# Recurrent mixer: row halves in turns into two banks, triangle inversions on GpSimd, and the convolution norm over four token tiles

## The chip, the cores and the metric

One core of a Trainium2 chip runs the whole kernel. The metric is the device time of one execution in microseconds: the median of three runs before was 3958.29 us (3955.69 to 3967.6). The engines are TensorE (PE in the profile; PEld are its weight loads), VectorE (DVE), ScalarE (ACT), GpSimd (POOL) and SyncE (SP), which issues most DMAs. PSUM has eight banks into which TensorE writes; the kernel names them by use.

## The reference, cut to what matters

Three blocks follow one another on a sequence of 1024 tokens of width 1024: four mixers, then a recurrent mixer (RWKV-7) beside a convolution group and a feed-forward layer, then a gated block with dilated attention. The change lies in the second block, between its input projection and its output projection.

```python
def rwkv7_recurrence(r, decay, k, v, a_vec, b_vec):
    ...
    def step(S, inp):
        r_t, w_t, k_t, v_t, a_t, b_t = inp
        sa = jnp.einsum('bhvk,bhk->bhv', S, a_t)
        S = S * w_t[:, :, None, :] + sa[..., :, None] * b_t[:, :, None, :] + v_t[..., :, None] * k_t[:, :, None, :]
        y = jnp.einsum('bhvk,bhk->bhv', S, r_t)
        return S, y
    ...

def conformer_conv_group(u, conv_w, conv_b, conv_ln_g, conv_ln_b):
    h = u[..., :D_CONV] * jax.nn.sigmoid(u[..., D_CONV:])
    h = lax.conv_general_dilated(...) + conv_b
    mu = jnp.mean(hf, axis=-1, keepdims=True)
    var = jnp.mean(jnp.square(hf - mu), axis=-1, keepdims=True)
    hn = (hf - mu) * lax.rsqrt(var + LN_EPS) * conv_ln_g + conv_ln_b
    return jax.nn.silu(hn).astype(u.dtype)
```

The recurrence has 8 heads of 64 channels and one state of 64x64 for each head. The kernel doesn't step through the 1024 tokens: it works in chunks of 64, for which the updates inside a chunk become a unit lower triangular system.

## The kernel before, in words

The large projections (helper line L251) are float32 products made of three calls on split operands. The recurrent stage uses plain float32 calls of `nc.tensor.matmul`; the trace shows each as two matmul instructions, called two passes here.

The stage takes eight token blocks j of 128 tokens, two chunks of 64 each. 512 channels stand as 4 pairs of 128 partitions; a head has 64 of them, so two heads share a pair, one on partitions 0 to 63 and one on 64 to 127 (the row halves). Five generators make the work of a block:

- `rwkv_prep(j)` loads r, k and v, makes the decay and the gate (L1336: products with `wup` on either row half into bank s; GpSimd L1340 to L1385), scales the operands, and forms the masked products of both chunks, `gs` (L1403 on TensorE, L1405 on VectorE), four groups of four calls, a group for each chunk and row half. Its ten work tiles `wk` are there once, so one block's preparation follows the other's.
- `rwkv_solve(j)` inverts the 16x16 triangles on the diagonal. DMAs bring them from `gs` through DRAM into a tile of 64 lanes by 256; GpSimd copies it (L1423) and sets the diagonal (L1424); then 14 steps, each a product (L1428) and a sum (L1430) of 14 to 56 elements a lane, each waiting for the one before; a transposing copy (L1433); and DMAs bring the result back as T16 and P16.
- `rwkv_pre(j)` transposes (L1457), forms ET from `gs` and T16 (L1465), takes three steps of a series with P16 (L1473) between which x1 is made (L1480), and ends with VU (L1488) and X (L1493). Each product is eight calls of 64 columns for each of the two chunks, each chunk on its own row half.
- `rwkv_chain(j)` carries the state through both chunks (L1516 to L1541), with Sc on GpSimd (L1518), and `rwkv_out(j)` normalises the output O (scaled on GpSimd in L1564) and gates it.

`rwkv` weaves chain(i), out(i-1), pre(i+1), solve(i+2) and prep(i+3) for i from -3 to 8, by the counts in `RW`; at i = -3 the generator `conv_ln` is woven in, which normalises the convolution output in eight tiles of 128 tokens (L1212 to L1234): transposes into a bank t, statistics on VectorE, a chain of small VectorE operations for the inverse root (L159 to L168), the normalisation out of the bank (L1221), transposes back, ScalarE, and two GpSimd operations. Weaving sets the order in which instructions are written; the framework's scheduler then reorders them by its own estimate of times. 88 filler products (L172) keep their places in the program order.

Banks: mm and o have one each, f (fillers) one, s two, t three. Products of `rwkv_prep` go to s, those of `rwkv_pre` and the norm's transposes to t.

## Time and profile before

| | |
|---|---|
| median of three runs | 3958.29 us |
| the profiled execution, its own time | 3958.3 us |
| its span | 3956.6 us |
| PE busy in the span | 3795.8 us (96%) |
| DVE, ACT, POOL busy | 2112.9 (53%), 1231.0 (31%), 540.1 us (14%) |
| the stage of the change in the span | 1116 to 1491 us |

A row of the chain gives shares of the span along the chain of work that ended last. A row of the stretches gives busy times and instruction counts in a window, and the granted clock of TensorE as a share of full speed (1.00 is 2.4 GHz). A row of waits names the waiting engine and line, and what released it. A timeline row gives start, duration, engine, line, operation, output and inputs, and in brackets idle time before it. Busy times of TensorE in a group of lines count each instruction from start to end, though instructions overlap. In the stage, inversion steps and work tiles share names, since their memory is cut out of weight tiles: "ws" and "kb" are such cuts.

### The profile page before, as it was taken

How to read it: one execution, taken by the hardware profiler on the slowest of the kernel's cores; microseconds unless marked ns; L12 is line 12 of the kernel's file. 1: busy time of each engine (PE TensorE's matmuls, PEld its weight loads, DVE VectorE, ACT ScalarE, POOL GpSimd, SP SyncE). 2: the span in 40 equal slices, each digit the busy share in tenths (PEclk: the TensorE clock that was granted, in tenths of full speed). 3: DMA queues.
4: the chain of work that ended last, by engine and by line, in shares of the span. 5: the costliest groups of instructions: out<-in, count | busy, mean ns of one | idle time of the engine just before them, and what ended most of it. 6: DMA issues, size and time to landing. Idle time of an engine off the chain costs nothing.

```text
span 3956.6 us, 52689 instructions
## 1 busy us (share of the span) xinstructions
PE 3795.8 (96%) x20288; PEld 3149.7 (80%) x20288; DVE 2112.9 (53%) x4845; ACT 1231.0 (31%) x2521; POOL 540.1 (14%) x825
## 2 busy tenths in 40 slices
PE   7999999799988989999999999999999999999998
PEld 6788888687867777888888888878788888888887
DVE  5356568678977865544444554444433443433155
ACT  4444435542233334222212242333322111121232
POOL 1011124300033411000000011111101211210000
PEclk9999998899978999999999999999999999999999
DMA  5321342431211133111111132111133222211143
GB/s 148 122 65 51 82 138 65 150 114 57 91 55 38 40 104 120 48 54 43 54 43 54 54 121 60 41 58 54 54 107 96 62 64 58 78 49 43 59 150 127
DMA packets 318636, 303.75 MB, mean 77 GB/s; under 512 B 50670, under 2 KB 260402, under 8 KB 318386
## 3 DMA queue, kind: packets, MB, share of 16 engines
q1 hardware_dynamic: 318386, 300.39, 24.5%
q8 instruction: 160, 2.62, 0.3%
q14 instruction: 90, 0.74, 0.1%
HBM read 234.27 MB, written 61.34 MB: 75 GB/s over the span
## 4 chain that ended last, share of the span: by engine, by line
PE 87%; DVE 6%; DMA 3%; ACT 1%; issue 1%; SPq 1%; POOL 1%; DVEq 0%; ACTq 0%; POOLq 0%
PE mm L251 71%; PE s L1809 2%; DMA wraw<-in_w_in_dram 1%; PE s L532 1%; PE t L568 1%; PE o L1831 1%; PE s L1990 1%; PE o L1883 1%; DVE ws L738 1%; PE t L213 1%; PE o L578 1%; PE o L579 1%; SPq L1439 1%; PE s L1403 0%; PE s L531 0%
## 5 line engine op out<-in xcount | busy, mean ns | idle before, releaser
L251 PE MATMUL mm<-ahi,whi 128*128 128x512 f32 x2464 | 967.2, 394 | 0.0
L251 PE MATMUL mm<-alo,whi 128*128 128x512 f32 x2464 | 965.5, 392 | 1.3 <-DVE alo L218 1.3
L251 PE MATMUL mm<-ahi,wlo 128*128 128x512 f32 x2464 | 964.3, 392 | 1.9 <-DVE wlo L184 1.9
L184 DVE TENSOR_TENSOR wlo<-wraw,whi 128x1024 fp32r<-128x1024 f32 (+2 forms) x300 | 358.2, 1231 | 361.1 <-PE mm L251 337.6
L251 PEld LDWEIGHTS mm<-ahi,wlo 128*128 128x128 f32 x2464 | 464.7, 189 | 98.4 <-DVE wlo L184 2.6
L251 PEld LDWEIGHTS mm<-ahi,whi 128*128 128x128 f32 x2464 | 465.8, 189 | 96.3 <-issue 0.4
L251 PEld LDWEIGHTS mm<-alo,whi 128*128 128x128 f32 x2464 | 465.1, 189 | 96.7 <-DVE alo L218 2.2
L183 ACT ACTIVATE whi<-wraw 128x1024 fp32r<-128x1024 f32 (+2 forms) x300 | 302.9, 1055 | 760.2 <-DMA wraw<-in_w_ff_dram 315.1
L251 PE MATMUL mm<-whi,ahi 128*128 128x512 f32 (+2 forms) x1088 | 400.2, 371 | 21.1 <-ACT whi L183 8.2
L251 PE MATMUL mm<-whi,alo 128*128 128x512 f32 (+2 forms) x1088 | 399.0, 368 | 1.6 <-DVE alo L218 1.6
L251 PE MATMUL mm<-wlo,ahi 128*128 128x512 f32 (+2 forms) x1088 | 400.4, 368 | 0.1
L251 PEld LDWEIGHTS mm<-whi,ahi 128*128 128x128 f32 x1088 | 206.6, 190 | 57.1 <-ACT whi L183 8.7
L1683 DVE TENSOR_TENSOR xm<-xm,mm 128x512 f32<-128x512 f32 x256 | 173.6, 684 | 119.8 <-PE mm L251 119.5
L251 PEld LDWEIGHTS mm<-wlo,ahi 128*128 128x128 f32 x1088 | 206.5, 190 | 35.2 <-issue 3.8
L251 PEld LDWEIGHTS mm<-whi,alo 128*128 128x128 f32 x1088 | 206.0, 189 | 35.2 <-issue 2.5
L251 PE MATMUL mm<-whi,ah 128*128 128x512 f32 x512 | 202.3, 395 | 0.0
L251 PE MATMUL mm<-wlo,ah 128*128 128x512 f32 x512 | 202.1, 395 | 0.0
L251 PE MATMUL mm<-whi,al 128*128 128x512 f32 x512 | 202.1, 395 | 0.0
L1170 DVE SCALAR_TENSOR_TENSOR cva<-cvh,vecs,cva 128x1022 f32<-128x1022 f32 (+29 forms) x120 | 145.4, 1262 | 0.2
L1665 DVE TENSOR_TENSOR fr<-fr 128x512 f32<-128x512 f32 x64 | 44.4, 694 | 154.0 <-ACT fr L1664 154.0
L207 POOL TENSOR_SCALAR x<-x,rT 128x1024 f32<-128x1024 f32 x16 | 20.9, 1307 | 752.3 <-PE mm L251 676.8
L1815 POOL TENSOR_SCALAR mS<-mS,s 128x256 f32<-128x256 f32 x128 | 60.8, 478 | 405.2 <-DVE s L1814 337.8
(576 smaller groups left out, 5761.2 us busy)
## 6 DMA issues: line engine op xcount, KB each, us to landing
wraw<-in_w_in_dram SPq DMA_DIRECT2D x41, 1024.0 KB
wraw<-in_w_ff_dram SPq DMA_DIRECT2D x32, 1024.0 KB
wraw<-in_w_in_dram SPq DMA_DIRECT2D x59, 512.0 KB
wraw<-in_w_out_dram SPq DMA_DIRECT2D x24, 1024.0 KB
gv<-go SPq DMA_DIRECT2D x32, 256.0 KB
vl<-gv SPq DMA_DIRECT2D x16, 512.0 KB
wraw<-in_w_proj_a_dram SPq DMA_DIRECT2D x8, 1024.0 KB
wraw<-in_w_proj_b_dram SPq DMA_DIRECT2D x8, 1024.0 KB
```

The source lines that it names most:

```text
L183: nc.scalar.activation(hi, src, AF.Copy)
L184: nc.vector.tensor_tensor(lo, src, hi.bitcast(F32), op=OP.subtract)
L213: nc.tensor.transpose(q[:, 128 * j:128 * j + 128], xn[:, (k + j) * 128:(k + j + 1) * 128], self.ident)
L251: nc.tensor.matmul(out, lhs[a][:, kl, ls], rhs[b][:, kr, rs], start=first and n == 0, stop=last and n == tot - 1)
L532: nc.tensor.matmul(q[:, :b - a], self.Q[0:64, h, qs], kl, start=False, stop=True)
L568: nc.tensor.transpose(t[:w, (2 * j + s) * 128:(2 * j + s + 1) * 128], Ps[s][:, k:k + w], c.ident)
L578: nc.tensor.matmul(o[:, :256], v[:w, 0:128], ph[:w, sl], start=first, stop=last, skip_group_check=True)
L1170: nc.vector.scalar_tensor_tensor(a[:, 30 - j:], h[:, 0:994 + j], wj, a[:, 30 - j:], op0=OP.mult, op1=OP.add)
L1665: nc.vector.tensor_tensor(r, r, r, op=OP.mult)
L1683: nc.vector.tensor_tensor(xm[t][:, ns], xm[t][:, ns], q, op=OP.add)
L1809: nc.tensor.matmul(q[:, :256], qk[:, a, qcol], qk[:, b, kcol], start=n == 0, stop=n == 2)
L1815: nc.gpsimd.tensor_scalar(S_, S_, r, 1.0, op0=OP.mult, op1=OP.mult)
```

## The change

Three edits, all in the second block. First, six kinds of products of `rwkv_prep` and `rwkv_pre` (wup, gs, ET, x1, VU with X) take two banks at once and are written so that calls on rows 0 to 63 and on rows 64 to 127 follow in turns, each half into its own bank. x1 of both chunks is made after the first step of the series, where chunk 1's stood after the second. Second, the 28 inversion steps of a block and the copy behind them are issued on GpSimd instead of VectorE. Third, `conv_ln` takes four token tiles at a time: their transposed values are copied to SBUF by ScalarE, their variances collected in one tile, one inverse root is taken for four, and the normalisation runs in place in SBUF. The weave count of the norm rises from 16 to 24.

```diff
@@ -1128,7 +1128,7 @@
 
 
 FN = 384
-RW = dict(chain=(9, "010000"), out=(4, "0000"), pre=(15, "100111011010001"), solve=(10, ""), prep=(7, "00010000001"), ln=16, weave=1)
+RW = dict(chain=(9, "010000"), out=(4, "0000"), pre=(15, "100111011010001"), solve=(10, ""), prep=(7, "00010000001"), ln=24, weave=1)
 
 
 class Block2:
@@ -1203,37 +1203,46 @@
                 yield
 
     def conv_ln(self, tmp):
+
         c, nc = self.c, self.c.nc
         g, b = c.vecs["conv_ln_g"], c.vecs["conv_ln_b"]
-        for t in range(8):
-            ts = slice(t * 128, t * 128 + 128)
-            q = c.psum("t")
-            for i in range(4):
-                nc.tensor.transpose(q[:, 128 * i:128 * i + 128], self.cv[:, i, ts], c.ident)
-            yield
-            st = c.sm([128, 6], pool=tmp)
-            nc.vector.bn_stats(st, q)
-            mv = c.sm([128, 2], pool=tmp)
-            nc.vector.bn_aggr(mv, st)
-            rs = c.sm([128, 1], tag="cl", pool=tmp)
-            c.rsqrt(rs, mv[:, 1:2], 1.0, 1e-5, "cl", tmp)
-            x = tmp.tile([128, 512], F32, tag="O", name=c.nm("lnx"), bufs=2)
-            nc.vector.tensor_scalar(x, q, mv[:, 0:1], rs, op0=OP.subtract, op1=OP.mult)
-            yield
-            q = c.psum("t")
-            yf = tmp.tile([128, 512], F32, tag="Pc", name=c.nm("lny"), bufs=3)
-            y = yf.rearrange("p (i t) -> p i t", i=4)
-            for i in range(4):
-                nc.tensor.transpose(q[:, 128 * i:128 * i + 128], x[:, 128 * i:128 * i + 128], c.ident)
-            for i in range(4):
-                nc.scalar.activation(y[:, i], q[:, 128 * i:128 * i + 128], AF.Identity, bias=b[:, i:i + 1], scale=g[:, i:i + 1])
-            yield
-
-            nc.scalar.activation(x, yf, AF.Tanh, scale=0.5)
-            nc.gpsimd.tensor_scalar(x, x, 0.5, 0.5, op0=OP.mult, op1=OP.add)
-            nc.gpsimd.tensor_tensor(yf, yf, x, op=OP.mult)
-            nc.sync.dma_start(self.catT[512:1024, ts].rearrange("(i p) t -> p i t", p=128), y)
-            yield
+        for t0 in (0, 4):
+            xs = []
+            mv = c.sm([128, 4, 2], tag="cmv", bufs=2, pool=tmp)
+            for k in range(4):
+                ts = slice((t0 + k) * 128, (t0 + k) * 128 + 128)
+                q = c.psum("t")
+                for i in range(4):
+                    nc.tensor.transpose(q[:, 128 * i:128 * i + 128], self.cv[:, i, ts], c.ident)
+                x = tmp.tile([128, 512], F32, tag="XO"[k % 2], name=c.nm("lnx"), bufs=2)
+                nc.scalar.activation(x, q, AF.Copy)
+                st = c.sm([128, 6], pool=tmp)
+                nc.vector.bn_stats(st, q)
+                nc.vector.bn_aggr(mv[:, k], st)
+                xs.append(x)
+                yield
+            rs = c.sm([128, 4], tag="cl", pool=tmp)
+            vr = c.sm([128, 4], tag="cl", pool=tmp)
+            nc.vector.tensor_copy(vr, mv[:, :, 1])
+            c.rsqrt(rs, vr, 1.0, 1e-5, "cl", tmp)
+            for k, x in enumerate(xs):
+                ts = slice((t0 + k) * 128, (t0 + k) * 128 + 128)
+                nc.vector.tensor_scalar(x, x, mv[:, k, 0:1], rs[:, k:k + 1], op0=OP.subtract, op1=OP.mult)
+                q = c.psum("t")
+                yf = tmp.tile([128, 512], F32, tag="Pc", name=c.nm("lny"), bufs=3)
+                y = yf.rearrange("p (i t) -> p i t", i=4)
+                for i in range(4):
+                    nc.tensor.transpose(q[:, 128 * i:128 * i + 128], x[:, 128 * i:128 * i + 128], c.ident)
+                for i in range(4):
+                    nc.scalar.activation(y[:, i], q[:, 128 * i:128 * i + 128], AF.Identity, bias=b[:, i:i + 1],
+                                         scale=g[:, i:i + 1])
+                yield
+
+                nc.scalar.activation(x, yf, AF.Tanh, scale=0.5)
+                nc.gpsimd.tensor_scalar(x, x, 0.5, 0.5, op0=OP.mult, op1=OP.add)
+                nc.gpsimd.tensor_tensor(yf, yf, x, op=OP.mult)
+                nc.sync.dma_start(self.catT[512:1024, ts].rearrange("(i p) t -> p i t", p=128), y)
+                yield
 
 
 
@@ -1329,11 +1338,14 @@
         for i, d in enumerate((r, k, v)):
             nc.sync.dma_start(r4(d), self.p2T[512 * i:512 * i + 512, js].rearrange("(r p) t -> p r t", p=128))
         sg, a, cs, kk, e, ei, ea, t1, t2, t3 = self.wk[:10]
-        for x, rows, b in ((sg, slice(0, 64), "w0"), (a, slice(64, 128), "a0")):
-            q = c.psum("s")
-            for pr in range(4):
-                ps = slice(128 * pr, 128 * pr + 128)
+
+        half = [slice(0, 64), slice(64, 128)]
+        qq = [c.psum("s") for _ in half]
+        for pr in range(4):
+            ps = slice(128 * pr, 128 * pr + 128)
+            for q, rows in zip(qq, half):
                 nc.tensor.matmul(q[:, ps], self.wup[rows, 0, ps], self.lwa[rows, js], start=True, stop=True)
+        for x, q, b in ((sg, qq[0], "w0"), (a, qq[1], "a0")):
             for pr in range(4):
                 ps = slice(128 * pr, 128 * pr + 128)
                 nc.scalar.activation(x[:, ps], q[:, ps], AF.Tanh, bias=self.hb[:, 4 * (b == "a0") + pr:4 * (b == "a0") + pr + 1], scale=0.5)
@@ -1396,12 +1408,12 @@
 
         for b in range(2):
             m = self.mG[:, b].rearrange("p i t -> p (i t)").unsqueeze(1).to_broadcast([128, 4, 128])
-            for s in range(2):
-                rs = slice(64 * s, 64 * s + 64)
-                q = c.psum("s")
-                for pr in range(4):
+            qq = [c.psum("s") for _ in half]
+            for pr in range(4):
+                for q, rs in zip(qq, half):
                     nc.tensor.matmul(q[:, 128 * pr:128 * pr + 128], kb[rs, pr, 2 * b:2 * b + 2], va[rs, pr, 1 + 4 * b:3 + 4 * b],
                                      start=True, stop=True)
+            for s, q in enumerate(qq):
                 TT(gs[:, b, s:8:2], r4(q), m, op=OP.mult)
                 yield
 
@@ -1425,12 +1437,12 @@
         for t in range(1, 15):
             x = lX[:, :t * (15 - t)].rearrange("p (i j) -> p i j", j=t)
             sh = [64, 15 - t, t]
-            nc.vector.tensor_tensor(x, mv[:, t + 1:16, t:t + 1].to_broadcast(sh), tv[:, t:t + 1, 0:t].to_broadcast(sh),
+            nc.gpsimd.tensor_tensor(x, mv[:, t + 1:16, t:t + 1].to_broadcast(sh), tv[:, t:t + 1, 0:t].to_broadcast(sh),
                                     op=OP.mult)
-            nc.vector.tensor_tensor(tv[:, t + 1:16, 0:t], tv[:, t + 1:16, 0:t], x, op=OP.add)
+            nc.gpsimd.tensor_tensor(tv[:, t + 1:16, 0:t], tv[:, t + 1:16, 0:t], x, op=OP.add)
             if t % 2:
                 yield
-        nc.vector.tensor_copy(lTT.rearrange("p (j t) -> p j t", t=16), tj)
+        nc.gpsimd.tensor_copy(lTT.rearrange("p (j t) -> p j t", t=16), tj)
         for i, (src, dst) in enumerate(((lT, T16), (lTT, P16))):
             nc.sync.dma_start(L[1 + i], src)
             for par in range(2):
@@ -1458,11 +1470,12 @@
                 nc.scalar.activation(dst, q, AF.Copy)
                 yield
         x1 = tmp.tile([128, 512], F32, tag="X1", name=c.nm("X1"), bufs=1)
-        for b in range(2):
-            ca = slice(64 * b, 64 * b + 64)
-            q = c.psum("t")
-            for h in range(8):
-                nc.tensor.matmul(q[Bh(b), H(h)], gs[Bh(b), b, h, ca], T16[Bh(b), h], start=True, stop=True)
+
+        qq = [c.psum("t") for _ in range(2)]
+        for h in range(8):
+            for b, q in enumerate(qq):
+                nc.tensor.matmul(q[Bh(b), H(h)], gs[Bh(b), b, h, 64 * b:64 * b + 64], T16[Bh(b), h], start=True, stop=True)
+        for b, q in enumerate(qq):
             TT(ET[Bh(b), :, Bh(b)], h8(q[Bh(b)]), self.mLow[Bh(b)].unsqueeze(1).to_broadcast([64, 8, 64]), op=OP.mult)
             yield
         cur = P0 = P16.rearrange("p h t -> p (h t)")
@@ -1474,23 +1487,28 @@
             cur = tmp.tile([128, 512], F32, tag="Pc", name=c.nm("Pc"), bufs=3)
             TT(cur, q, P0, op=OP.add)
             yield
-            if i < 2:
-                q = c.psum("t")
+            if i == 0:
+                qq = [c.psum("t") for _ in range(2)]
                 for h in range(8):
-                    nc.tensor.matmul(q[Bh(i), H(h)], gs[Kh(i), i, h, Kh(i)], VU[i][Kh(i), H(h)], start=True, stop=True)
-                nc.scalar.activation(x1[Bh(i)], q[Bh(i)], AF.Copy)
-                yield
+                    for b, q in enumerate(qq):
+                        nc.tensor.matmul(q[Bh(b), H(h)], gs[Kh(b), b, h, Kh(b)], VU[b][Kh(b), H(h)], start=True, stop=True)
+                for b, q in enumerate(qq):
+                    nc.scalar.activation(x1[Bh(b)], q[Bh(b)], AF.Copy)
+                    yield
         X = self.X[j] = tmp.tile([128, 512], F32, tag="X", name=c.nm("X"), bufs=2)
-        for b in range(2):
-            q = c.psum("t")
-            for h in range(8):
-                pr, s = h // 2, h % 2
+        qq = [c.psum("t") for _ in range(2)]
+        for h in range(8):
+            pr, s = h // 2, h % 2
+            for b, q in enumerate(qq):
                 nc.tensor.matmul(q[H(s), H(pr)], VU[b][Bh(b), H(h)], cur[Bh(b), H(h)], start=True, stop=True)
+        for b, q in enumerate(qq):
             nc.scalar.activation(va[:, :, 3 + b], q[:, 0:256].rearrange("p (r t) -> p r t", r=4), AF.Copy)
             yield
-            q = c.psum("t")
-            for h in range(8):
+        qq = [c.psum("t") for _ in range(2)]
+        for h in range(8):
+            for b, q in enumerate(qq):
                 nc.tensor.matmul(q[Bh(b), H(h)], cur[Bh(b), H(h)], x1[Bh(b), H(h)], start=True, stop=True)
+        for b, q in enumerate(qq):
             nc.scalar.activation((X if j or b else VU[b])[Bh(b)], q[Bh(b)], AF.Copy)
             yield
 
```

The scheduler decides what of the turns remains. On TensorE in the first preparation, the gs products (L1403 before, L1414 after; s are banks, one name for each taking) stand so before, among the norm's transposes:

```order
L1227 MATMUL t_10921<-ident,lnx_10919 128x128 x4
L1403 MATMUL s_11109<-va_10864,kb_10868 128x128 x4
L1403 MATMUL s_11115<-va_10864,kb_10868 128x128 x4
L1212 MATMUL t_11016<-ident,cva_9085 128x128 x4
L1403 MATMUL s_11121<-va_10864,kb_10868 128x128 x4
L1227 MATMUL t_10988<-ident,lnx_10966 128x128 x4
L1403 MATMUL s_11127<-va_10864,kb_10868 128x128 x4
```

Each group of four calls has its own bank, and other work lies between two of them. After, the same place on TensorE, from the fifth call on:

```order
L1414 MATMUL s_11197<-va_10864,kb_10868 128x128
L1414 MATMUL s_11198<-va_10864,kb_10868 128x128
L1414 MATMUL s_11197<-va_10864,kb_10868 128x128
L1414 MATMUL s_11198<-va_10864,kb_10868 128x128
L1235 MATMUL t_10962<-ident,lnx_10888 128x128 x4
L1235 MATMUL t_10982<-ident,lnx_10898 128x128 x4
L1235 MATMUL t_10997<-ident,lnx_10929 128x128 x4
L1414 MATMUL s_11209<-va_10864,kb_10868 128x128 x4
L1414 MATMUL s_11210<-va_10864,kb_10868 128x128 x4
```

The first two groups go in turns now, a call each; the next two (s_11209, s_11210) have moved behind the norm's transposes as blocks of four calls.

On TensorE at the end of the last block's pre step, VU (L1488, after L1503) and X (L1493, after L1510) stand so before:

```order
L1576 MATMUL mm_14572<-lora,wup 128x128 x4
L1488 MATMUL t_14552<-Pc_14547,ws_10870 64x64 x8
L1493 MATMUL t_14562<-X_2722_14385,Pc_14547 64x64 x8
L1488 MATMUL t_14579<-Pc_14547,ws_10870 64x64 x8
L251 MATMUL mm_14810<-whi_14837,ahi_14742 128x512
L251 MATMUL mm_14823<-whi_14837,ahi_14742 128x512
L1493 MATMUL t_14589<-X_2722_14385,Pc_14547 64x64 x8
```

VU and X of one chunk come before those of the other, in blocks of eight. After, the same place on TensorE, from VU's thirteenth call on:

```order
L1503 MATMUL t_14492<-Pc_14487,ws_10870 64x64
L1503 MATMUL t_14493<-Pc_14487,ws_10870 64x64
L1503 MATMUL t_14492<-Pc_14487,ws_10870 64x64
L1503 MATMUL t_14493<-Pc_14487,ws_10870 64x64
L1510 MATMUL t_14519<-X_2694_14325,Pc_14487 64x64 x8
L251 MATMUL mm_14750<-whi_14777,ahi_14682 128x512
L251 MATMUL mm_14763<-whi_14777,ahi_14682 128x512
L1510 MATMUL t_14520<-X_2694_14325,Pc_14487 64x64 x8
```

VU's sixteen calls go in turns between both banks; X's are two blocks of eight calls, as before.

On GpSimd, around the inversion of an early block, the queue before holds only the copy and the diagonal of the inversion (L1423, L1424) between the preparation's lines:

```order
L1423 COPY ws_10872<-ws_10870 64x256
L1385 TENSOR_TENSOR ws_10873<-ws_10873,ws_10871 128x512
L1234 TENSOR_TENSOR lny_11270<-lny_11270,lnx_11267 128x512
L1424 MEMSET ws_10872 64x16
L1345 TENSOR_SCALAR ws_10871<-rk_11823,vecs_625 128x128 x4
L1340 TENSOR_SCALAR ws_10871<-ws_10871 128x512
L1361 TENSOR_TENSOR ws_10871<-ws_10871,s_2369_11926 128x512
L1423 COPY ws_10872<-ws_10870 64x256
L1424 MEMSET ws_10872 64x16
```

Of the inversion there are two rows a block. After, on GpSimd at the end of such an inversion (L1440 and L1442 are its steps, L1445 its copy; the next inversion has begun with L1435 and L1436 on the other half of the lanes):

```order
L1440 TENSOR_TENSOR ws_10874<-ws_10870,ws_10872 64x26
L1442 TENSOR_TENSOR ws_10872<-ws_10872,ws_10874 64x2x13
L1352 TENSOR_SCALAR ws_10871<-ws_10871 128x512
L1440 TENSOR_TENSOR ws_10874<-ws_10870,ws_10872 64x14
L1435 COPY ws_10872<-ws_10870 64x256
L1358 TENSOR_SCALAR ws_10873<-ws_10871,vecs_625,ka_10855 128x128 x3
L1442 TENSOR_TENSOR ws_10872<-ws_10872,ws_10874 64x14
L1358 TENSOR_SCALAR ws_10873<-ws_10871,vecs_625,ka_10855 128x128
L1373 TENSOR_TENSOR ws_10871<-ws_10871,s_2342_11875 128x512
L1436 MEMSET ws_10872 64x16
L1440 TENSOR_TENSOR ws_10874<-ws_10870,ws_10872 64x14
L1445 COPY kb_10868<-ws_10872 64x256
```

The preparation's L1352, L1358, L1373, L1389 and L1397 and the chain's Sc (L1536) now stand between and behind the steps.

## Rows read from the trace of the kernel before

**Rows 1.** Chain on the page: share of the span by engine
```profile
PE 87%; DVE 6%; DMA 3%; ACT 1%; issue 1%; SPq 1%; POOL 1%; DVEq 0%; ACTq 0%; POOLq 0%
```

**Rows 2.** Stretches: from and to, length, busy us of each engine, clock, DMA.
```profile
core 0: us, PE busy (x) PEld busy (x) DVE busy (x) ACT busy (x) POOL busy (x), PEclk, DMA share, GB/s
1116.00:1224.00 108.00, 85.66 (x573) 69.21 (x571) 81.94 (x211) 42.92 (x106) 50.53 (x65) 0.62 0.21 54
1224.00:1436.00 212.00, 189.41 (x2386) 159.41 (x2385) 170.76 (x435) 78.37 (x171) 72.31 (x98) 0.92 0.21 52
1297.00:1329.00 32.00, 31.22 (x421) 26.64 (x421) 28.06 (x70) 13.26 (x32) 15.67 (x20) 1.00 0.23 48
...
1436.00:1491.00 55.00, 43.35 (x483) 36.52 (x483) 25.72 (x60) 19.64 (x35) 10.05 (x9) 0.90 0.31 92
1491.00:1560.00 69.00, 69.00 (x304) 56.77 (x305) 39.44 (x84) 25.88 (x47) 4.49 (x4) 0.96 0.45 156
```

**Rows 3.** TensorE's waits, 1116 to 1491: total us, times, longest.
```profile
PE t L1457 <- ACT ws L1458: 10.2, 3, 7.1
PE t L1227 <- DVE lnx L1221: 9.9, 3, 4.9
PE mm L1568 <- POOL O L1564: 6.7, 1, 6.7
```

**Rows 4.** TensorE's timeline, five places: start us, duration us, line, instructions.
```profile
1137.69 2.07 PE L1403 MATMUL s<-va,kb 64*128 64x128 f32 x8
...
1285.91 1.16 PE L1403 MATMUL s<-va,kb 64*128 64x128 f32 x8 [0.57 <-DVE kb L1388]
...
1346.87 1.14 PE L1480 MATMUL t<-ws,gs 64*64 64x64 f32 x16
...
1359.05 1.71 PE L1403 MATMUL s<-va,kb 64*128 64x128 f32 x16
1360.68 0.68 PE L1488 MATMUL t<-Pc,ws 64*64 64x64 f32 x16
```

**Rows 5.** Groups by line, VectorE, 1116 to 1491: busy us, mean ns.
```profile
L1430 DVE TENSOR_TENSOR ws<-ws,ws 64x14 f32<-64x14 f32 (+6 forms) x112 | 30.4, 271 | 2.5
L1428 DVE TENSOR_TENSOR ws<-ws,ws 64x14 f32<-64x14 f32 (+6 forms) x112 | 27.4, 245 | 13.0 <-POOL ws L1423 10.8
...
L1405 DVE TENSOR_TENSOR gs<-s,mG 128x512 f32<-128x512 f32 x32 | 21.8, 684 | 14.7 <-PE s L1403 14.5
...
L164 DVE SCALAR_TENSOR_TENSOR cl<-cl,cl 128x1 f32<-128x1 f32 x24 | 10.4, 432 | 0.1
...
L168 DVE SCALAR_TENSOR_TENSOR cl<-cl,cl 128x1 f32<-128x1 f32 x24 | 9.0, 374 | 0.2
```

**Rows 6.** VectorE's timeline, first and last of the 29 operations of one inversion.
```profile
1231.23 0.17 DVE L1428 TENSOR_TENSOR ws<-ws,ws 64x14 f32<-64x14 f32 x1 [6.54 <-POOL ws L1423]
...
1241.13 0.37 DVE L1433 COPY kb<-ws 64x256 f32<-64x256 f32 x1
```

**Rows 7.** One line's instructions on GpSimd: ns min/median/max, first and last start.
```profile
L1424 POOL MEMSET ws<- x8: 118/118/120, 1157.3 to 1407.4; 64x16 f32 x8
...
L1518 POOL TENSOR_TENSOR Sc<-Tc,ff x15: 607/776/1462, 1235.3 to 1461.9; 128x256 f32<-128x256 f32 x15
...
L1385 POOL TENSOR_TENSOR ws<-ws,ws x8: 1262/1268/1722, 1129.4 to 1386.1; 128x512 f32<-128x512 f32 x8
```

**Rows 8.** GpSimd's timeline, two operations that depend on each other.
```profile
1314.12 0.61 POOL L1423 COPY ws<-ws 64x256 f32<-64x256 f32 x1
1314.79 0.12 POOL L1424 MEMSET ws<- 64x16 f32 x1
```

**Rows 9.** VectorE's timeline, one small step of the norm twice.
```profile
1143.82 1.26 DVE L164 SCALAR_TENSOR_TENSOR cl<-cl,cl 128x1 f32<-128x1 f32 x1
...
1145.30 0.22 DVE L164 SCALAR_TENSOR_TENSOR cl<-cl,cl 128x1 f32<-128x1 f32 x1
```

**Rows 10.** GpSimd's timeline at the first of these.
```profile
1143.80 1.26 POOL L1234 TENSOR_TENSOR lny<-lny,lnx 128x512 f32<-128x512 f32 x1
```

## The prediction

> **What bounds the kernel now.** I read the chain of the page first, then the stretches, the waits of TensorE, and single instructions. The chain is TensorE's for 87% of the span [rows 1]: elsewhere a microsecond off another engine buys nothing. The changed lines run only between 1116 and 1491 us, so the stretches [rows 2] are cut there. In the opening (1116 to 1224, three preparations, two solves and the convolution norm) TensorE is busy 85.66 of 108 us, at a granted clock of 0.62, and VectorE 81.94: neither alone is the limit, they wait for each other. From 1224 to 1436 six token blocks pass in 212 us, 35.3 us a block; TensorE is busy 189.41 and idle 22.6, clock 0.92. In the tail (1436 to 1491) 11.65 of 55 are idle. From 1491 TensorE is busy 69.00 of 69 us, and the instructions there keep their order: what the stage gives up moves everything behind it forward one for one, and nothing behind it can hide a loss. So TensorE's work in the stage counts nearly fully, and beside it the idle 22.3 + 22.6 + 11.65 = 56.6 us. Its largest waits [rows 3] are for the copies behind the pre step's transposes (10.2 us), for VectorE's normalisation in the norm (9.9, in the opening) and for GpSimd's scaling of O (6.7).
>
> **Products on opposite halves.** A float32 call is two passes. Eight passes of the products L1403 alone take 1.16 us at full clock; two groups of opposite row halves in a row take 1.71 for sixteen [rows 4], not 2.3: the end of one block overlaps the start of the next. So opposite halves do run at once. The price of full alternation is not in the trace. Bound: no better than the one half alone, 1.16 for sixteen, so at most 0.55 less than adjacent blocks. For 64-column calls there is a nearer row: sixteen passes into one quadrant take 1.14 us (L1480), sixteen in turns into two column halves 0.68 (L1488) [rows 4]: 0.46 a group. The lower bound is zero, should row halves not do what column halves do.
>
> What is really alternated, the order of instructions tells: calls that follow one on the other bank of the pair are, of all eight blocks, before and after, 13 and 40 for gs (of 128), 2 and 17 for the wup products (of 64), 4 and 65 for ET, none and 8 for x1, none and 120 for VU, none and 1 for X (of 128 each). The scheduler has sorted X back into blocks, and most of x1 and wup. Worked out: gs, some four pairs of groups in full turns, 4 x 0.55 = 2.2 us. Wup, where adjacent blocks and a pair or two in turns replace scattered calls, 2 us. ET, half of the eight blocks, two groups of sixteen each: 4 x 2 x 0.46 = 3.7. x1, eight adjacent pairs, at half of a group's price: 8 x 0.23 = 1.8. VU already alternates column halves; opposite rows on top, between 0 and 0.46, I take 0.25 x 8 = 2. X nothing. Sum 11.7 us at full clock, and some 1.5 more where the opening runs at half clock (eight passes of L1403 take 2.07 there [rows 4]). That is about 1.5 us in each middle block, 1.7 with the switches between groups that go. Bounds for a block: 0, and with everything in turns 2 x 0.55 + 0.96 (wup) + 3 x 0.94 (ET, x1, X) + 0.46 = 5.3.
>
> Two banks taken at once come out of the same pools (s has two banks, t three), and a second group must wait for its bank before the first can finish its turns. The waits on t now are the 10.2 and part of the 9.9 us above; a pair leaves one bank of t for everything else. I cost that at nothing, since the scheduler puts other calls between; without that cover it is one eviction, 0.68 us on VectorE (L1405 [rows 5]), for each of three pairs a block: 2 us.
>
> **Inversions to GpSimd, VectorE's side.** The 224 steps take VectorE 30.4 + 27.4 = 57.8 us [rows 5], 7.2 a block of 28.06 busy in an undisturbed one (1297 to 1329 [rows 2]). Some of the stage's waits are for VectorE's queue, in which the inversion stands between evictions. Off it, the evictions behind products come sooner. That is the reason for the gain in idle time, not the 57.8 us themselves.
>
> **GpSimd's side.** The trace has no such step there. Nearest rows [rows 7]: a memset of 64x16 takes 118 ns, a two-input operation of 128x256 607 at least, one of 128x512 1262. The steps have 14 to 56 elements a partition. Lower end 28 x 0.118 = 3.3 us, upper 28 x 0.607 = 17. I take 0.25 a step, just over the line between the first two rows at 56 elements (0.20): 7.0. A dependent step starts 60 ns after the one before (1314.12 + 0.61 to 1314.79 [rows 8]): 28 x 0.06 = 1.7. So 9 us alone; with other work in the queue 11 to 13. On VectorE the least disturbed inversion lasts from 1231.23 to 1241.13, 9.9 us [rows 6]; the others have more evictions between. GpSimd, without evictions, need not be the later one.
>
> What it pushes: GpSimd is busy 15.67 of an undisturbed 32 us [rows 2]; with 9 it is 25. Behind the inversion in its queue stand, by the order and with the line numbers after, the next preparation's L1352, L1358, L1373, L1389 and L1397, the chain's Sc (L1536), and the scaling of O (L1582), for which TensorE already waits once [rows 3]. The limit: 35.3 - 15.7 for its own work, and some 5 for its waits, leaves 15 us an inversion; beyond that GpSimd sets the pace.
>
> The Trainium skill, page "GPSIMD Engine Reference", section "4.1 Engine selection", speaks against the move: it sends two-input elementwise work to VectorE and calls GpSimd about twice as slow. The trace agrees for large tiles (1262 ns on GpSimd [rows 7], 684 on VectorE [rows 5], both on 128x512). By that rule an inversion would cost twice VectorE's 7.2, some 14.5 us, just under the limit worked out above; the 9 us of idle time would not be won, and the sum would be -22 instead of -31.
>
> **Norm over four tiles.** VectorE loses eight small rsqrt chains, of which the six long steps a tile cost 10.4 + 9.0 = 19.4 us [rows 5], and gets two chains for four tiles, some 20 steps of about 0.22 [rows 9], 4.4 us. Those 432 and 374 ns are inflated: the same step takes 1.26 us at 1143.82 and 0.22 at 1145.30 [rows 9], and the long one starts 20 ns behind a GpSimd multiplication of the same 1.26 us [rows 10]. So beside a two-input GpSimd operation VectorE can be held for its whole length. New are eight copies on ScalarE, 42.92 of 108 us busy [rows 2], which has room. The first normalised tile comes later, since four statistics are awaited; the transposes behind it (9.9 us of waits) then come in fours. Between nothing and all 9.9 us of that wait.
>
> **The sum**, against the profiled execution (3958.3 us, span 3956.6, the median of the runs within 0.1). Opening: -8 (the 9.9 of waits, 3 of products, less 5 for two inversions on a GpSimd with 50.53 us of work there; bounds -20 and +8). Middle: 6 x 1.7 = 10 of products and 9 of the 22.6 idle, -19 (bounds -32 = 6 x 5.3, and +12 = 6 x 2 for banks). Tail: -4, two blocks' products and a last inversion without evictions between (bounds -10, +5). Together -31: **3927 us**.
>
> **Rivals.** *GpSimd becomes the pace* (slower). For: 25 of 32 us busy before any disturbance, and operations of VectorE on two SBUF tiles may hold it, as [rows 9] and [rows 10] show it the other way round. VectorE's other work is 28.06 - 7.2 = 20.9 us a block; if half of that holds the inversion, 9 + 10.5 gives some 20 us. Against: that needs it to fall inside the inversion, a third of the block. From 15 us it decides; at 20, 6 x 5 = +30, less 4 in the opening: 3984. The Trainium skill, page "SBUF — State Buffer", section "Who interferes with whom", says it as a rule: a VectorE instruction with two SBUF inputs and a GpSimd instruction reading SBUF exclude each other, the first blocks the other. By that rule both the steps and the preparation's VectorE work stretch; rows 9 and 10 agree.
>
> *No change.* The preparations share one set of work tiles and run one behind the other; if their serial chain sets the 35.3 us and the scheduler's blocks give up most of the products, only the opening's waits and some products are left: -8, 3950. For: X, x1 and wup are sorted back. Against: TensorE is busy 31.22 of 32 us in an undisturbed block [rows 2], so there its work is the pace.
>
> *More than forecast.* Adjacent blocks overlap anyway, and cheaper inversions let idle time go: 8 x 5.3 = 42 of products or 25 of products and 30 of the idle: 3905. Against: the counts above.
>
> **How the numbers follow.** Forecast 0.55 (its own range 3908 to 3946), GpSimd the pace 0.14, no change 0.19 (3942 to 3958), more 0.12 (3888 to 3908). The range 3892 to 3972 leaves out most of the slow rival and the end of the fast one. 0.3%, 12 us, is about what a measurement of this kernel can tell from no change. Faster by more: 0.53 + 0.12 + 0.04 = 0.69; within: 0.13 + 0.02 + 0.03 = 0.18; slower: 0.13.
>
> **What would show it.** In the trace after: GpSimd's inversion steps near 0.25 us and 11 to 13 us from first to last; TensorE's busy time from 1116 on some 13 us less; its waits for L1221's successor gone; the stretch behind the stage unchanged but 31 us earlier. Wrong if steps take 0.4 us or more, if TensorE's largest waits are then for GpSimd, or if products in turns take as long as in blocks.

## The result: 3919.61 us, and the profile after

The changed kernel takes 3919.61 us (median of four runs, 3917.31 to 3924.8) against 3960.18 of the kernel before (four runs): ratio 0.9901, 95% interval 0.9888 to 0.9915, 40.6 us less. The forecast was 3927. The profiled execution took 3917.31 us, its span is 3915.6, 41.0 less than before. The stretches of the changed kernel, cut at the same points of the work as [rows 2] (columns as there):

```profile
core 0: us, PE busy (x) PEld busy (x) DVE busy (x) ACT busy (x) POOL busy (x), PEclk, DMA share, GB/s
...
1116.00:1206.00 90.00, 65.84 (x591) 54.31 (x589) 61.56 (x114) 47.38 (x118) 69.12 (x122) 0.73 0.25 63
1206.00:1398.00 192.00, 179.19 (x2369) 153.39 (x2368) 145.69 (x260) 77.12 (x167) 132.96 (x272) 0.92 0.24 59
1398.00:1455.00 57.00, 45.85 (x483) 38.59 (x481) 26.44 (x60) 19.50 (x35) 11.07 (x11) 0.89 0.27 89
1455.00:1524.00 69.00, 69.00 (x308) 56.94 (x309) 39.68 (x86) 26.25 (x48) 4.50 (x4) 0.97 0.46 157
```

The opening went from 108 to 90 us, the middle from 212 to 192, the tail from 55 to 57: 36 us of the 41 are the stage's. Behind it TensorE is again busy for 69.00 of 69 us. The other 5 lie outside, most of them (4.3 us of busy time) in one stretch of the third block, whose instructions are the same; the granted clock there is 0.99 instead of 0.98. Executions of the kernel before alone lie between 3951 and 3968 us over all comparisons, so I make nothing of those 5.

TensorE's largest waits in the stage, after (total us, times, longest), beside [rows 3]:

```profile
PE s L1405 <- POOL ws L1389: 9.8, 3, 8.7
PE t L1216 <- DVE s L1220: 4.4, 2, 3.6
PE mm L1586 <- POOL O L1582: 4.2, 1, 4.2
...
PE t L1235 <- DVE lnx L1230: 1.4, 1, 1.4
```

The 9.9 us for the normalised tile are 1.4 now, and the 10.2 for the copies behind the transposes are gone. The largest wait is now for GpSimd (L1389, a product of the preparation): 8.7 us of it at once, in the opening. The products on TensorE's timeline, as in [rows 4]:

```profile
1133.50 2.08 PE L1414 MATMUL s<-va,kb 64*128 64x128 f32 x16 [2.22 <-DVE cl L167]
...
1192.44 1.16 PE L1414 MATMUL s<-va,kb 64*128 64x128 f32 x16
...
1199.78 0.69 PE L1503 MATMUL t<-Pc,ws 64*64 64x64 f32 x32
1200.31 1.09 PE L1510 MATMUL t<-X,Pc 64*64 64x64 f32 x16
```

Sixteen passes of gs in full turns take 1.16 us, as long as eight alone; at half clock 2.08. VU's 32 take 0.69 instead of two times 0.68. X takes 1.1 us a half, as before. Last, the steps of an inversion on GpSimd, by line from 1116 to 1455 (columns as in [rows 5]) and on the timeline:

```profile
L1440 POOL TENSOR_TENSOR ws<-ws,ws 64x14 f32<-64x14 f32 (+6 forms) x112 | 36.0, 322 | 7.4
L1442 POOL TENSOR_TENSOR ws<-ws,ws 64x14 f32<-64x14 f32 (+6 forms) x112 | 35.8, 320 | 8.0
```

```profile
1385.77 1.11 POOL L1442 TENSOR_TENSOR ws<-ws,ws 64x26 f32<-64x26 f32 x1
1386.96 1.11 POOL L1440 TENSOR_TENSOR ws<-ws,ws 64x36 f32<-64x36 f32 x1
1388.14 1.12 POOL L1442 TENSOR_TENSOR ws<-ws,ws 64x36 f32<-64x36 f32 x1
...
1393.56 0.28 POOL L1440 TENSOR_TENSOR ws<-ws,ws 64x56 f32<-64x56 f32 x1
1393.92 0.30 POOL L1442 TENSOR_TENSOR ws<-ws,ws 64x56 f32<-64x56 f32 x1
```

Undisturbed a step takes 0.28 us and the next begins 0.08 after it; three here take 1.11.

### The profile page after: what moved, and what is told of

Its sections match the earlier page's. It is cut to its first block, busy times and chain, and to the rows that moved or that the text cites. A ratio compares the mean times of both kernels' runs of the same rounds, so it can differ in the third digit from the quotient of the medians.

```text
span 3915.6 us, 52651 instructions
## 1 busy us (share of the span) xinstructions
PE 3764.2 (96%) x20288; PEld 3128.5 (80%) x20288; DVE 2069.0 (53%) x4573; ACT 1234.1 (32%) x2529; POOL 624.8 (16%) x1057
## 4 chain that ended last, share of the span: by engine, by line
PE 63%; DVE 2%; DMA 1%; ACT 0%; POOL 0%; issue 0%; SPq 0%; DVEq 0%; ACTq 0%; POOLq 0%
PE mm L251 55%; PE s L1827 2%; DMA wraw<-in_w_in_dram 1%; PE s L2008 1%; PE o L1849 1%; PE o L1901 1%; PE t L1894 0%; PE t L1486 0%; PE t L213 0%; PE t L1926 0%; PE t L1871 0%; PE s L1414 0%; PE t L1494 0%; DMA catT<-y 0%; PE o L1557 0%
## 5 line engine op out<-in xcount | busy, mean ns | idle before, releaser
L184 DVE TENSOR_TENSOR wlo<-wraw,whi 128x1024 fp32r<-128x1024 f32 (+2 forms) x300 | 358.5, 1232 | 360.4 <-PE mm L251 336.8
L251 PE MATMUL mm<-whi,ahi 128*128 128x512 f32 (+2 forms) x1088 | 400.3, 371 | 20.7 <-ACT whi L183 7.9
L1170 DVE SCALAR_TENSOR_TENSOR cva<-cvh,vecs,cva 128x1022 f32<-128x1022 f32 (+29 forms) x120 | 145.4, 1262 | 0.2
```

The costliest lines, as they stand in the source:

```text
L184: nc.vector.tensor_tensor(lo, src, hi.bitcast(F32), op=OP.subtract)
L251: nc.tensor.matmul(out, lhs[a][:, kl, ls], rhs[b][:, kr, rs], start=first and n == 0, stop=last and n == tot - 1)
L1170: nc.vector.scalar_tensor_tensor(a[:, 30 - j:], h[:, 0:994 + j], wj, a[:, 30 - j:], op0=OP.mult, op1=OP.add)
```

## Experiments: each part alone, and each left out

The theory is that the three parts act on different costs: products on TensorE's work, inversions on VectorE's queue, the norm on the opening. Its rivals are that one part carries it, or that the parts need each other. Six kernels hold one or two of the parts; their edits are pieces of the diff above.

**Inversions alone** (on the kernel before; the copy behind them too):

```diff
-            nc.vector.tensor_tensor(x, mv[:, t + 1:16, t:t + 1].to_broadcast(sh), ...
+            nc.gpsimd.tensor_tensor(x, mv[:, t + 1:16, t:t + 1].to_broadcast(sh), ...
```

> The kernel before with one part of the change alone: the 28 inversion steps and their copy on GpSimd; products and norm as before. Theory A (the parts add up as in the prediction: 13 us of TensorE work from the products, the idle time of the middle stretch from the inversions, the opening from the norm): about 3958 - 10 = 3948 us, from TensorE's idle time between the opening and the tail, with TensorE's busy time in the stage within 4 us of before; the opening no shorter than before by more than 4 us. Rival B (the inversion leaving VectorE is what shortens the opening, since two inversions of 20 us lie in it between other VectorE work): 3958 - 20 = 3938 us or less, with the first chain step 10 to 15 us earlier. Rival C (GpSimd becomes the pace when nothing else is eased): 3958 or slower.

**Products alone:** the diff's hunks in `rwkv_prep` and `rwkv_pre`, of the kind

```diff
+        for h in range(8):
+            for b, q in enumerate(qq):
+                nc.tensor.matmul(q[Bh(b), H(h)], gs[Bh(b), b, h, 64 * b:64 * b + 64], T16[Bh(b), h], start=True, stop=True)
```

> The kernel before with the products of opposite row halves in turns into two banks alone; inversions on VectorE and norm as before. Theory A: TensorE's busy time in the stage falls by 12 to 15 us and the time by about as much, 3958 - 13 = 3945 us. Rival: in the middle stretch TensorE's work isn't what counts as long as the inversions stand in VectorE's queue; work goes down and idle time up by as much, 3953 to 3960 us.

**Norm alone:** `conv_ln` and `ln`.

```diff
-        for t in range(8):
+        for t0 in (0, 4):
```

> The kernel before with the convolution norm over four token tiles alone (and its weave count). Theory A: the opening gains 8 to 18 us, nothing after it changes: 3958 - 12 = 3946 us, the first chain step 8 to 18 us earlier. Rival B: the norm's waits are replaced by the wait for inversion 0, which ends where it ended before: 3955 to 3960 us, first chain step within 4 us of before.

**Without the inversions** (back on VectorE):

```diff
-            nc.gpsimd.tensor_tensor(x, mv[:, t + 1:16, t:t + 1].to_broadcast(sh), ...
+            nc.vector.tensor_tensor(x, mv[:, t + 1:16, t:t + 1].to_broadcast(sh), ...
```

> The changed kernel with the inversions and their copy back on VectorE (products and norm as changed). Theory A (parts add): it loses the inversions' 10 us, 3920 + 10 = 3930 us, the loss as idle time of TensorE in the middle stretch. Rival B (the inversion is what lets the other two gain): it loses 20 us or more, 3940 us or slower, opening included. Rival C (GpSimd's inversions cost as much as they give): 3920 us or faster.

**Without the norm** (tile by tile again):

```diff
-        for t0 in (0, 4):
+        for t in range(8):
```

> The changed kernel with the norm as it was before (tile by tile, its weave count too). Theory A (the norm is what a lengthened opening pays back; with the products it gave nothing, since inversion 2 then starts 20 us behind its gs on VectorE, and it is the inversions on GpSimd that cure this): 8 to 10 us slower than the changed kernel, 3928 to 3932 us, the first chain step 8 us later. Rival B (the norm over four tiles costs more than it gives beside the two other parts): 3910 to 3920 us, no slower than the changed kernel.

**Without the products** (one bank after the other again):

```diff
-        qq = [c.psum("t") for _ in range(2)]
-        for h in range(8):
-            for b, q in enumerate(qq):
+        for b in range(2):
+            q = c.psum("t")
+            for h in range(8):
```

> The changed kernel with the products as before (one bank after the other, row halves in blocks). Theory A (TensorE's work is what the middle stretch consists of): 12 to 16 us slower than the changed kernel, 3932 to 3936 us, with TensorE 12 us busier in the stage. Rival (the products' turns are hidden behind the inversions and the pool of banks): within 4 us of the changed kernel, 3916 to 3924.

Measured, against the kernel before in the same comparison (3958.92, 3958.87), and the stretches of the profiled execution:

| parts | median us | ratio, 95% interval | opening, middle, tail us |
|---|---|---|---|
| none | 3958.9 | | 108, 212, 55 |
| inversions | 3945.17 | 0.997 (0.9959 to 0.9981) | 106, 185, 63 |
| products | 3933.03 | 0.9935 (0.9923 to 0.9948) | 95, 211, 56 |
| norm | 3947.59 | 0.9969 (0.9957 to 0.9981) | 104, 209, 52 |
| products, norm | 3943.51 | 0.9959 (0.9945 to 0.9972) | 104, 201, 56 |
| products, inversions | 3938.58 | 0.9946 (0.9934 to 0.9958) | 115, 184, 55 |
| inversions, norm | 3934.81 | 0.9937 (0.9925 to 0.9949) | 94, 196, 64 |
| all | 3919.61 | 0.9901 (0.9888 to 0.9915) | 90, 192, 57 |

Alone the parts are worth 13.7 (inversions), 25.9 (products) and 11.3 us (norm); on top of the two others 23.9, 15.2 and 19.0. Taking the inversions back cost over 20 us, the opening included, as rival B had it. Leaving out the products cost what its theory A said (12 to 16), leaving out the norm twice what its theory A said (8 to 10).

Inversions alone and the norm alone came at the times of their theories A (3948 and 3946), but not in their way. With the inversions TensorE's busy time in the stage fell by 9 us (318.4 to 309.5), where no more than 4 was expected, and the norm shortened the opening by 4 us, not by 8 to 18. Inversions shorten middle and tail together (267 to 248 us).

Products alone gave twice what was expected. In the profiled execution (3939.38 us, the slowest of its five) all of the stage's 13 us are in the opening, 6 more lie outside the stage, and middle and tail together stay at 267. That is the time that their rival had there, but not its reason: TensorE's busy time in the middle did not go down, it went up, from 189.41 us to 193.22, at a granted clock of 0.87 instead of 0.92 [rows 2]. The middle with products alone, then with inversions alone:

```profile
1212.00:1423.00 211.00, 193.22 (x2371) 163.95 (x2369) 175.16 (x433) 76.25 (x166) 74.84 (x95) 0.87 0.23 54
1227.00:1412.00 185.00, 176.82 (x2368) 151.01 (x2369) 137.66 (x253) 75.81 (x165) 120.84 (x250) 0.98 0.25 60
```

With the inversions off VectorE the products do shorten middle and tail (248 to 239, and with the norm 260 to 249); with the inversions on VectorE they do so by 4 us at most (267 to 267, and with the norm 261 to 257).

Two pairs came out slower than products alone, which no theory of mine foresaw: with the norm by 10 us (runs from 3934.7 to 3949.18 against 3931.6 to 3939.38), with the inversions by 5 (3931.45 to 3944.8). The runs overlap, so the first is likely and the second is not shown. Every edit also lets the scheduler order the whole stage anew, so a few us of each row may be the order's and not the part's.

For products with inversions, what is lost against the changed kernel is in the opening (115 us against 90). GpSimd's timeline there, inversion 0 (L1431 and L1433, its copy L1436) among the old norm's L1233 and L1234:

```profile
1153.23 0.61 POOL L1431 TENSOR_TENSOR ws<-ws,ws 64x14 f32<-64x14 f32 x1
1153.81 1.26 POOL L1376 TENSOR_TENSOR ws<-ws 128x512 f32<-128x512 f32 x1
1155.03 1.26 POOL L1234 TENSOR_TENSOR lny<-lny,lnx 128x512 f32<-128x512 f32 x1
...
1189.12 0.61 POOL L1233 TENSOR_SCALAR lnx<-lnx 128x512 f32<-128x512 f32 x1
...
1192.30 1.27 POOL L1234 TENSOR_TENSOR lny<-lny,lnx 128x512 f32<-128x512 f32 x1
...
1195.52 0.61 POOL L1436 COPY kb<-ws 64x256 f32<-64x256 f32 x1
```

From first step to copy it takes 42 us; in the changed kernel it goes from 1152 to 1175. **The norm's two GpSimd operations moved to VectorE** in this kernel tests whether that is the reason:

```diff
-            nc.gpsimd.tensor_scalar(x, x, 0.5, 0.5, op0=OP.mult, op1=OP.add)
-            nc.gpsimd.tensor_tensor(yf, yf, x, op=OP.mult)
+            nc.vector.tensor_scalar(x, x, 0.5, 0.5, op0=OP.mult, op1=OP.add)
+            nc.vector.tensor_tensor(yf, yf, x, op=OP.mult)
```

> Products in turns and inversions on GpSimd with the norm tile by tile (as in e_prod_inv), but the norm's two GpSimd operations a tile (0.61 and 1.26 us) on VectorE. Theory A (what the norm over four tiles gives beside the two other parts is GpSimd's queue: inversion 0 takes from 1153 to 1187 us there, with the norm's and the preparation's operations between its steps, and its copy comes at 1196; in the changed kernel 1152 to 1174): inversion 0 ends some 10 us earlier, the opening falls from 115 to 100 us or less, 3938 - 12 = 3926 us. Rival B (it is VectorE's small chains and the waits for the normalised tile): VectorE gets 8 to 10 us more to do, the opening stays at 113 us or more, 3938 us or slower.

It takes 3925.36 us (ratio 0.9913, 0.9899 to 0.9926), 13 us less; the copy starts at 1170.36 and the opening is 105 us:

```profile
1117.00:1222.00 105.00, 82.41 (x592) 66.35 (x590) 78.33 (x175) 45.64 (x113) 63.63 (x125) 0.63 0.23 56
```

So theory A holds in its core: with the inversions on GpSimd, the old norm is in GpSimd's way. It doesn't cover all: 105 us lie between what A (100 or less) and B (113 or more) had, and the opening is still 15 us longer than the changed kernel's, although inversion 0 is ready earlier than there. These 15 us are not idle time of TensorE (22.6 us here, 24.2 there). They are its busy time, 82.41 us against 65.84 for as many instructions, at a granted clock of 0.63 instead of 0.73. No run isolates why the clock is lower here. The whole kernel is 6 us slower than the changed one, in runs that overlap (3920.88 to 3928.37 against 3917.31 to 3924.8).

For products with norm, the trace shows inversion 2 late: it starts at 1232, with products alone at 1211, though its gs ended at 1211. Its first copy L1435 stands on GpSimd behind the next preparation's L1389:

```profile
1224.49 1.27 POOL L1385 TENSOR_TENSOR ws<-ws 128x512 f32<-128x512 f32 x1 [1.43 <-ACT ws L1384]
1227.86 1.28 POOL L1389 TENSOR_TENSOR ws<-rk,rk 128x512 f32<-128x512 f32 x1 [2.10 <-PE o L1538]
1229.09 1.08 POOL L1435 COPY ws<-ws 64x256 f32<-64x256 f32 x1
```

That this place in the queue is what costs the pair its gain is argued from the trace; no run isolates it.

## Experiments: turns, banks, and GpSimd's limit

**Blocks instead of turns**, all six products, banks and x1 as changed:

```diff
-        for h in range(8):
-            for b, q in enumerate(qq):
+        for b, q in enumerate(qq):
+            for h in range(8):
```

> The changed kernel, with both banks of each pair still taken at once and x1 still made after the first step, but each half's calls written as a block. Theory A (the turns are what the products give: gs pairs 1.16 instead of 1.71 us, VU pairs 0.69 instead of 1.36, ET 1.2 instead of 2.1): 10 to 14 us slower than the changed kernel, 3930 to 3934 us, TensorE busier by the same. Rival (taking two banks and the moved x1 give the scheduler its freedom, the turns little): within 4 us, 3916 to 3924.

It takes 3936.59 us (ratio 0.9947, 0.9935 to 0.9959), 17 us more than the changed kernel, where 10 to 14 were expected. TensorE in its middle stretch is 12.5 us busier:

```profile
1211.00:1407.00 196.00, 191.67 (x2382) 162.95 (x2382) 138.38 (x265) 77.47 (x171) 132.14 (x259) 0.91 0.23 57
```

The middle is only 4 us longer for it, since TensorE's idle time there falls from 12.8 to 4.3; the opening is 4 us longer (94), the tail 9 (66). The turns are what the products give: this kernel is no faster than the one without that part (3934.81).

**One bank** for both halves of ET, x1 and X, three places:

```diff
-        qq = [c.psum("t") for _ in range(2)]
+        qq = [c.psum("t")] * 2
```

> The changed kernel, but ET, x1 and X put both halves into one bank t (they lie on different partitions of it) instead of two; VU, gs and wup keep two. Theory A (the scheduler sorted X and x1 back into blocks because the second bank wasn't free when the first half was ready, so with one bank the turns stay): X pairs in about 1.2 instead of 2.1 us and x1 pairs likewise, 8 x 1.8 = 14 us of TensorE less, of which some 10 to 12 count: 3907 to 3911 us. Rival (two halves cannot run at once into one bank, or the wait is for the operands, not the bank): X and x1 still 1.14 us a half, 3916 to 3924 us.

It takes 3906.23 us (3904.37 to 3908.21; ratio 0.9866, 0.9853 to 0.9879): 13 us less than the changed kernel and 53 less than before, the fastest of all, as theory A had it. X's 32 passes take 1.10 us, x1's sixteen 0.68:

```profile
1204.15 1.10 PE L1510 MATMUL t<-X,Pc 64*64 64x64 f32 x32
...
1274.54 0.68 PE L1494 MATMUL t<-ws,gs 64*64 64x64 f32 x16
```

The middle stretch:

```profile
1210.00:1388.00 178.00, 164.29 (x2379) 134.84 (x2377) 135.08 (x264) 76.43 (x168) 129.45 (x259) 0.93 0.26 62
```

Two halves on different partitions of one bank run at once. What undid the turns of X and x1 was the second bank. Not all of the 13 us need be theirs: by line, X takes TensorE 8.8 us instead of 20.1, x1 14.6 instead of 20.7, and ET, which the edit changes too, 13.8 instead of 16.9. VU, in two banks, has its turns in both kernels. Why the scheduler keeps them there and not in X, no run isolates.

**One bank, inversions on VectorE:**

```diff
-            nc.gpsimd.tensor_tensor(x, mv[:, t + 1:16, t:t + 1].to_broadcast(sh), ...
+            nc.vector.tensor_tensor(x, mv[:, t + 1:16, t:t + 1].to_broadcast(sh), ...
```

> The kernel with one bank for ET, x1 and X, but inversions and copy back on VectorE. If GpSimd's inversions are worth what they are in the changed kernel (3943.5 against 3919.6, 24 us): 3928 to 3932 us. If less of TensorE's work makes the rest count more: slower than 3935. If they were only worth their 14 us of the kernel before: 3916 to 3922.

It takes 3934.24 us (ratio 0.9938, 0.9926 to 0.9951), between the first expectation and the second. The inversions on GpSimd are worth 28 us with one bank and 24 with two; the one bank is worth 13 us with them on GpSimd and 9 with them on VectorE (3943.51 to 3934.24). So the two gains nearly add up, and the 4 us between are within the spread of the runs. In the middle stretch TensorE is 15 us busier than with one bank and GpSimd, at a granted clock of 0.88 instead of 0.93, and idle for 25.5 us instead of 13.7:

```profile
1214.00:1419.00 205.00, 179.50 (x2381) 148.11 (x2380) 176.90 (x440) 77.34 (x171) 76.90 (x98) 0.88 0.22 55
```

**Longer inversions:** each product step three times.

```diff
+            for _ in range(3):
-            nc.gpsimd.tensor_tensor(x, mv[:, t + 1:16, t:t + 1].to_broadcast(sh), ...
+                nc.gpsimd.tensor_tensor(x, mv[:, t + 1:16, t:t + 1].to_broadcast(sh), ...
```

> The changed kernel with each of the 14 product steps of an inversion issued three times on GpSimd (same values): 28 more dependent steps a block at 0.27 us and 0.08 between, 9.8 us, so an inversion of 22 to 24 us instead of 12.4 undisturbed. The rival from the prediction (GpSimd sets the pace from 15 us an inversion): 7 to 9 us a block over it in six blocks and more in the opening, 3965 to 3985 us. Theory A (GpSimd has room: busy 133 of 192 us in the middle, 22 a block, so 32 with the addition is just the period): half of the 9.8 us a block is seen, 3940 to 3960 us. If the inversion is hidden altogether: 3918 to 3925.

It takes 3969.07 us (ratio 1.0024, 1.0015 to 1.0032), more than before the change: 49 us for 8 x 9.8 = 78 us of steps. The opening and the middle:

```profile
1115.00:1241.00 126.00, 81.09 (x664) 67.45 (x663) 69.44 (x125) 51.77 (x129) 99.90 (x214) 0.67 0.21 53
1241.00:1442.00 201.00, 181.44 (x2296) 152.67 (x2294) 127.04 (x238) 72.97 (x153) 163.96 (x406) 0.91 0.21 51
```

36 of them are in the opening, where GpSimd is busy for 99.90 of 126 us, only 9 in the middle. The time is the rival's (3965 to 3985), the place is not: the rival had 7 to 9 us in each of the six blocks of the middle.

**Shorter inversions:** every second pair of steps left out.

```diff
-        for t in range(1, 15):
+        for t in range(1, 15, 2):
```

> The changed kernel with 7 of the 14 pairs of inversion steps left out (every second one; the triangles are then not inverted): an inversion of some 6.5 us instead of 12.4. If the inversion's length on GpSimd still sets a part of the stage: 6 us a block less in the opening and the tail at least, 3900 to 3910 us. If it is hidden beside TensorE's work (as I hold for the middle stretch, where TensorE is idle 2 us a block): 3914 to 3920 us.

It takes 3920.21 us (ratio 0.9899, 0.9884 to 0.9914), the changed kernel's time. The inversion's length on GpSimd is hidden as it is, and not if it nearly doubles. The rival of the prediction is real; where between these two lengths it begins, no run shows.

## Why the prediction was right, step by step

**One for one behind the stage:** right, 36 us of stage, TensorE full behind it.

**Products.** The mechanism was right, and the bound for full turns was met to the digit (1.16 for sixteen passes). The term was 13 us in all; measured are 15 (part left out) and 17 (blocks). But it was made up otherwise. By line, the kernel without the products against the changed one, TensorE spends 19.8 and 14.4 us on wup (5.4 less, where I had 2), 10.9 and 5.6 on VU (5.3, I had 2), 22.0 and 16.9 on ET (5.1, I had 3.7), 33.5 and 32.4 on gs (1.1, I had 2.2), 20.7 and 20.7 on x1 (nothing, I had 1.8), 17.8 and 20.1 on X (2.3 more, I had nothing). The lines of wup and VU, without the products, then changed:

```profile
L1345 PE MATMUL s<-lora,wup 64*128 64x128 f32 x128 | 19.8, 290 | 0.0
L1347 PE MATMUL s<-lora,wup 64*128 64x128 f32 x128 | 14.4, 285 | 0.0
L1497 PE MATMUL t<-Pc,ws 64*64 64x64 f32 x256 | 10.9, 224 | 0.5 <-DVE Pc L1484 0.5
L1503 PE MATMUL t<-Pc,ws 64*64 64x64 f32 x256 | 5.6, 224 | 2.5 <-DVE Pc L1488 2.5
```

VU I took at 0.25 a pair of groups, it is 1.36 - 0.69 = 0.67: opposite rows on top of column halves are worth as much again. And the opening, "some 1.5 more" at half clock: there eight passes took 2.07 [rows 4] and sixteen in turns take 2.08, and products alone shortened the opening by 13 us. TensorE's busy time in the stage fell by 27 us (318.4 to 290.9) and not by 13: 20 of them in the opening.

**Two banks at once, costed at nothing.** For waits this did no harm: the 10.2 us for the copies behind the transposes are gone, and the new waits for a bank t are smaller (4.4 us in the norm's transposes L1216, 2.3 before x1, 1.2 before X). The sum also had X at nothing and x1 at half a price already, since the order showed them in blocks. What it missed is that the second bank is the cause: one bank gives X and x1 their turns, and the kernel 13 us.

**VectorE's side.** Taken were 9 of the 22.6 us of idle in the middle; it fell from 22.6 to 12.8. But not by shorter inversions: I had 11 to 13 us from first to last, the trace has 14 (the last one) to 28, where VectorE had 10 to 28. The 9 us alone became 10 (0.28 + 0.08 a step), the rest is other work in the queue and VectorE's operations. The run with half the steps shows that the length doesn't matter; what counts, by the runs with the inversions back on VectorE, is that VectorE's queue is free of them.

**GpSimd's limit,** 15 us in the middle by my sum: there an addition of 9.8 us cost 1.5 a block, so the middle has more room than that. The limit is in the opening, which I had given 5 us for two inversions.

**Norm.** The waits I named went (9.9 to 1.4), though TensorE's idle time in the opening did not. What makes the norm worth 19 us beside the other parts is for 13 of them GpSimd's queue, a place the step did not look at.

**Opening, middle, tail.** The opening was forecast at -8 and came at -18, and not as the sum had it. TensorE's idle time there, which was to give the 9.9 us of waits, went from 22.3 to 24.2: other waits took the place of those that went. What fell is its busy time, 85.66 to 65.84, at a granted clock of 0.73 instead of 0.62. The middle was forecast at -19 and came at -20, and that is in part luck. The sum had 10 from products and 9 from idle time, but leaving the products out costs the middle only 4 us (196 against 192); alone they shorten it by 1, and the inversions alone by 27. The tail was forecast at -4 and came at +2; its idle time stayed at 11 us, and TensorE was 2.5 us busier. This was a wrong sign, and small.

**The signs I gave.** One sign of being wrong came true: TensorE's largest wait is for GpSimd (9.8 us, L1389). 8.7 us of it stand at once in the opening, and the opening was shorter all the same. The inversions are not what makes it long: with half their steps the opening takes 92 us, no less than the changed kernel's 90. The steps take 0.32 us on average, under the 0.4 that I had named, but not 0.25.

**The two pages.** The Trainium skill, page "GPSIMD Engine Reference", section "4.1 Engine selection" (twice as slow on GpSimd), holds for large tiles here (1262 ns against 684 [rows 7, rows 5]); for these small steps the ratio is 322 to 245 ns and 320 to 271 on average [rows 5], and the sum by that rule (-22) was the worse one. The rule of the Trainium skill in "SBUF — State Buffer", section "Who interferes with whom", is borne out in both directions, by the rows at the end.

## What to carry to other kernels

Products of half the rows should alternate halves, and into one bank if the outputs lie on different partitions: a second bank can make the scheduler put the halves back into blocks, as for X and x1 here, and what it did is read from the order and the timeline. A chain of small dependent steps can be better off on an engine where each step is slower (322 against 245 ns here), if it leaves a queue that others wait for. In these runs its own length counted only once the new engine was nearly full, and where that is (here the opening) is read from the stretch and not from the mean.

## What the runs showed of the hardware

A matmul pair on all four quadrants (VU: rows and columns in turns) runs at twice the rate of one that alternates columns only: 32 passes in 0.69 us, where sixteen took 0.68 before.

VectorE and GpSimd hold each other, and the one that begins second waits. The three steps of 1.11 us above lie beside one row of VectorE,

```profile
1385.53 3.62 DVE L1631 TENSOR_TENSOR alo<-alo,ahi 128x1024 fp32r<-128x1024 f32 x3
```

three operations of 1.2 us on two SBUF tiles each. The other way, the preparation's product on VectorE, before (L1376) and after (L1388):

```profile
L1376 DVE TENSOR_TENSOR rk<-rk,ws x8: 616/677/694, 1124.9 to 1383.1; 128x512 f32<-128x512 f32 x8
```

```profile
L1388 DVE TENSOR_TENSOR rk<-rk,ws x8: 679/1522/1997, 1124.5 to 1334.8; 128x512 f32<-128x512 f32 x8
```

Its median went from 677 to 1522 ns. The inversion steps are not what holds it: with the inversions on GpSimd and the products as before the median is 660. Six of the seven long ones began 0.02 to 0.07 us behind a GpSimd operation of the preparation or the norm on 128x512, as here:

```profile
1236.27 1.52 DVE L1388 TENSOR_TENSOR rk<-rk,ws 128x512 f32<-128x512 f32 x1 [0.37 <-POOL ws L1358]
```

```profile
1236.21 1.04 POOL L1373 TENSOR_TENSOR ws<-ws,s 128x512 f32<-128x512 f32 x1
```

In the kernel with products and norm VectorE once began first, by 0.03 us. There its product took 0.69 us and the GpSimd operation 1.79, where that line's median is 1.27:

```profile
1187.98 0.69 DVE L1388 TENSOR_TENSOR rk<-rk,ws 128x512 f32<-128x512 f32 x1
```

```profile
1188.01 1.79 POOL L1385 TENSOR_TENSOR ws<-ws 128x512 f32<-128x512 f32 x1 [2.18 <-ACT ws L1384]
```
